# A longer warming, a moved modulation and split products at the opening of a one-core transformer and state-space kernel

## The chip, the core and the metric

The kernel runs on one core of a Trainium2 chip. The metric is the device time of one execution in microseconds. Three runs of the kernel before took 1899.47, 1901.17 and 1896.9 us, with a median of 1899.47. In the text TensorE is PE in the profile (PEld is its loading of weights), VectorE is DVE, ScalarE is ACT, GpSimd is POOL, and the queue that issues the transfers is SP.

## The reference

The reference is a two-layer backbone over 512 latent tokens with a context of 256 tokens, model width 1024. Layer 0 mixes with grouped-query attention, layer 1 with a bidirectional state-space mixer, and a gated feed-forward layer with a short convolution follows each. Every sub-layer starts with a root-mean-square norm and a modulation (a shift and a scale that depend on a condition vector):

```python
silu_c = jax.nn.silu(c)
silu_cc = jax.nn.silu(c_ctx)
...
    mod_l = jnp.split((silu_c @ ada_w[i] + ada_b[i])[:, None, :], 6, axis=-1)
    mod_c = jnp.split(silu_cc @ ada_w[i] + ada_b[i], 6, axis=-1)
    h_l = modulate(rms_norm(x, norm_mix_w[i]), mod_l[0], mod_l[1])
    h_c = modulate(rms_norm(ctx, norm_mix_w[i]), mod_c[0], mod_c[1])
...
q_l, k_l, v_l = jnp.split(h_lat @ w_qkv, [Q_DIM, Q_DIM + KV_DIM], axis=-1)
```

The change touches only the first of these: the norm and modulation of the latent tokens and of the context in layer 0, and the products `h_lat @ w_qkv` for the first six blocks of 128 columns of queries and keys.

## The kernel before

Activations lie transposed: 1024 features are eight tiles of 128 partitions, and a tile has a column for each token, 512 of latents and 256 of context. Precision comes from splitting every operand into a high part of reduced precision (type fp32r) and a low part that is the rest. A product of two such operands is three matmuls, high by high, weight high by activation low and weight low by activation high (`mm3`, lines 105, 106 and 108). ScalarE makes a high part by a copy, and VectorE or GpSimd the low part by a subtraction (`split`, lines 85 and 87).

The function `attention` writes the order of TensorE, ScalarE and VectorE by hand for the opening; the engines run their instructions in the order of the code. The opening goes like this:

- Transfers are queued on SP: the latents X, the parameters, then for each of eight feature tiles a block of modulation weights (`wada`, 1 MB in three pieces) and a slab of projection weights (`wst`, 128 x 768), with a table of constants (`cst`, which holds the identity) and the context in between. SP's order follows the program and isn't changed by the diff.
- TensorE runs 24 products of a tile of ones (line 541, `warm`), whose result nobody reads. In the profile each 128 x 128 product of plain fp32 is two records.
- ScalarE squares the eight latent tiles, VectorE adds them to `acc`, and TensorE sums that over partitions (line 274, `ss`). `rstd_rows` then makes the reciprocal root by a logarithm and an exponential on ScalarE and small VectorE steps, spreads it to `rba` (line 285) and turns it by four transposes (line 291, `rsT`).
- `ada` makes the shift and scale of one feature tile in stages, at each `next`: eight products of 32 columns (line 128, `ps_ada`) and a copy of their result by VectorE (line 130, `ada_sb`); then two products that turn it (line 134, `ps_adt`), and in `modulation` two additions of 128 x 2 (line 145, `mod`) and the gain (line 148, `moda`). The bodies of `ada` and `modulation` aren't changed.
- `modulated` applies them: VectorE makes `ht` (line 319), ScalarE the high part `hha` (line 328), VectorE the low part `hla` (line 329).
- The main loop runs over eight k-steps m, one for each feature tile. A k-step is six products of 128 x 512 outputs in three parts each (`k_step`, 18 matmuls into six accumulators `ps_l`). In front of its first product stands ps_ada of tile m + 1; behind its second stand ps_adt, the modulation and `modulated` of tile m + 1. The slab of tile m + 1 is split in the k-step m, by ScalarE and, for the first seven, by GpSimd.
- The context's norm is woven in: in the k-steps 1 and 2 four squares each on ScalarE (line 584) with their adds on VectorE (line 586), ahead of the k-step's products; in k-step 3 the sum over partitions, in k-step 4 its transposes, ahead of the products; from k-step 4 on, two context tiles are modulated in each step behind its second product.

k-step 0 differs in one thing: its own modulation is made ahead of the loop, so TensorE waits there for hha. ps_ada of tile 1 stands in that wait.

Of the kernel before, what the change touches and what calls it, by code (L numbers as in the profile page):

```python
# [7 lines left out]
P = 128  # L8
F32 = mybir.dt.float32
F32R = mybir.dt.float32r  # L10
AF = mybir.ActivationFunctionType
ALU = mybir.AluOpType
# [3 lines left out]
D = 1024  # L16
KT = D // P
L = 512
C = 256
# [48 lines left out]
def t3(g, name, dt=F32, n=T):  # L68
    return g.t3p.tile([P, n], dt, tag="t3", bufs=g.n3, name=name)
# [195 lines left out]
def rstd_rows(g, sq, n, cols, width, name, bank):  # L265

    nc = g.nc
    c = cols.shape[-1]  # L270
    nt = n // P
    ps = bank(f"ss{name}")
    for t in range(nt):
        nc.tensor.matmul(ps[:, t * c : (t + 1) * c], sq[:, t * P : (t + 1) * P], cols, start=True, stop=True)
    small = lambda nm: g.p.tile([P, nt * c], F32, tag="rst", bufs=8, name=nm)
    a, y, u = small("rsa"), small("rsy"), small("rsu")
    nc.vector.tensor_scalar(a, ps[:, : nt * c], 1.0 / width, EPS, ALU.mult, ALU.add)

    for f in ((lambda: nc.scalar.activation(y, a, AF.Ln)), (lambda: nc.scalar.activation(y, y, AF.Exp, scale=-0.5))):
        follow(g, f()) if g.tables else f()  # L280
    nc.vector.tensor_tensor(u, y, a, ALU.mult)
    nc.vector.scalar_tensor_tensor(u, y, -0.5, u, ALU.mult, ALU.mult)
    rb = t3(g, f"rb{name}", n=n)
    wide = lambda v: v.unsqueeze(2).broadcast_to([P, nt * c, P // c])
    nc.vector.scalar_tensor_tensor(rb.rearrange("p (a b) -> p a b", b=P // c), wide(u), 1.5, wide(y), ALU.add, ALU.mult)
    yield BREAK
    out = []
    for t0 in range(0, nt, 4):
        pt = bank(f"rsT{name}")
        for t in range(t0, min(nt, t0 + 4)):  # L290
            nc.tensor.transpose(pt[:, (t - t0) * P : (t - t0 + 1) * P], rb[:, t * P : (t + 1) * P], g.ident)
        yield (pt, t0 * P, min(n, (t0 + 4) * P))
# [20 lines left out]
def modulated(g, hl, x, rs, a, b, layer, ca, cb, v, m, pool=False):  # L313

    nc = g.nc
    n = b - a
    t = t3(g, "ht", n=n)
    for ap, c0, c1 in parts(x[m], a, b):
        nc.vector.scalar_tensor_tensor(t[:, c0:c1], ap, g.moda[layer][ca][:, m, v : v + 1], rs[:, c0:c1],  # L319
                                       ALU.mult, ALU.mult)  # L320
    bias = g.mod[layer][cb][:, m, v : v + 1]
    hi, lo = (h[:, a:b] for h in hl)
    if pool:
        nc.scalar.activation(t, t, AF.Identity, bias=bias)
        nc.scalar.copy(hi, t)
        nc.gpsimd.tensor_tensor(lo, t, _r(hi), ALU.subtract)
        return
    nc.scalar.activation(hi, t, AF.Identity, bias=bias)
    nc.vector.scalar_tensor_tensor(lo, t, bias, _r(hi), ALU.add, ALU.subtract)
# [160 lines left out]
def attention(g, adas, project, X):  # L490


    nc, I = g.nc, g.I
    S64 = slice(0, 64), slice(64, 128)
    Bk, Sb = (lambda name: Bank(g, name)), (lambda name: S(g, name))
    t2 = lambda name, dt=F32: g.t3p.tile([P, 512], dt, tag="t2", bufs=6, name=name)
    g.h = [[htiles(g, n, f"a{i}_{m}") for m in range(KT)] for i, n in enumerate((L, C))]
    hl, hc = g.h
# [8 lines left out]
    slabs = []  # L507
# [29 lines left out]
                nc.sync.dma_start(X[:, a : a + 4, L:], I["ctxT"][a * P : (a + 4) * P].rearrange("(k p) t -> p k t", p=P))  # L537

    warm = Bk("warm")
    for _ in range(24):  # L540
        nc.tensor.matmul(warm[:, :P], g.ones, g.ones, start=True, stop=True)
    acc = t3(g, "acc", n=L)
    for m in range(KT):
        sq = t2("sql") if m else acc
# [14 lines left out]
                            e.rearrange("p (k v) -> p k v", v=2), ALU.mult)  # L559
    next(norm)  # L560
    next(mods[0])
    rsl, _, _ = next(norm)
    next(mods[0])
    next(loads[0], None)
# [6 lines left out]
    def k_step(m, j, out, h):  # L571
        ks = slice(j * P, (j + 1) * P)
        mm3(g, tuple(w[:, ks] for w in slabs[m]), [(out, h[m])], m == 0, m == KT - 1)

    for m in range(KT):
        if 1 <= m < KT - 5 + 1:
            next(mods[m + 5 - 1])
            next(loads[m + 5 - 1])
        if m == 1:
            sqc = t3(g, "sqc", n=C)  # L580
        if m in (1, 2):
            for a in range(4 * m - 4, 4 * m):
                sq = t2("sqc")[:, :C] if a else sqc
                nc.scalar.activation(sq, xs[1][a], AF.Square)
                if a:
                    nc.vector.tensor_tensor(sqc, sqc, sq, ALU.add)
        if m == 3:
            norm = rstd_rows(g, sqc, C, g.ones[:, :1], D, "a", Bk)
            next(norm)
        if m == 4:  # L590
            rsc = t3(g, "rsc", n=C)
            pt, _, _ = next(norm)
            nc.scalar.copy(rsc, pt[:, :C])
        for j in range(6):
            if m + 1 < KT and j == 0:
                next(mods[m + 1])
            k_step(m, j, pl[j], hl)
            if m + 1 < KT:
                if j == 0:
                    next(loads[m + 1], None)  # L600
                if j == 0 + 1:
                    next(mods[m + 1])
                    modulated(g, hl[m + 1], xs[0], rsl, 0, L, 0, 1, 0, 0, m + 1)
            if m >= 4 and j == 1:
                for a in (2 * m - 8, 2 * m - 7):
                    modulated(g, hc[a], xs[1], rsc, 0, C, 0, 1, 0, 1, a, pool=True)
    for _ in mods:
        next(_, None)
    man.__exit__(None, None, None)
# [1036 lines left out]
```

## Time and profile before

| what | value |
|---|---|
| runs, median of three | 1899.47 us (1896.9 to 1901.17) |
| the profiled execution | 1901.27 us |
| its span from first to last instruction | 1899.3 us |
| mean granted TensorE clock | 0.995 |
| TensorE busy, 0 to 10 us and 10 to 15 us | 7.40 and 3.13 us |
| first product of the k-steps 0, 1, 2 and 3 | 19.45, 28.15, 33.98, 41.50 us |

Everything in the prediction is read from one profiled execution. A row of the order in time gives the start, how long it took from the first to the last of a group, the engine, the line, the operation, the tile written and those read, and how often; in brackets stands the idle time ahead of it and what ended it. A row of a stretch gives its bounds and length and then, for each engine, its busy time and the number of instructions, at last the granted TensorE clock as a share of full speed, the share of the transfer engines and GB/s. Records of consecutive matmuls overlap: their distance from start to start is what one costs in a stream.

### The profile page before, as it was taken

What the parts mean: (1) busy time and instruction counts of PE and PEld (TensorE: products, weight loads), DVE (VectorE), ACT (ScalarE), POOL (GpSimd) and SP (SyncE); (2) the same over time, 40 slices, a digit from 0 to 9 for tenths busy, and PEclk for the clock granted to TensorE, in tenths of its full rate; (3) what the DMA queues carried; (4) which work ended last, traced back from release to release, by engine and by line L of the source; (5) the groups of instructions that cost most, each with busy time, mean ns of one, the idle gap of its engine ahead of it and who ended that gap; (6) DMA issues with size and microseconds to landing.
All of it is one profiled execution on the core that took longest, in us unless ns stands there. A gap on an engine that the chain in (4) does not pass through costs nothing.

```text
span 1899.3 us, 27264 instructions
## 1 busy us (share of the span) xinstructions
PE 1863.7 (98%) x10696; PEld 1526.5 (80%) x10696; DVE 1335.2 (70%) x1989; ACT 841.9 (44%) x1450; POOL 251.3 (13%) x236
## 2 busy tenths in 40 slices
PE   8999999989999999999989999999999999999999
PEld 6864545588888888888888888888888888888887
DVE  4588989678777777544488777777878576565655
ACT  3654544354122222222266777766667353323331
POOL 2200000031000000000040344443335200000000
PEclk8999999999999999999999999999999999999999
DMA  9223341014433555222123444444344323323232
GB/s 340 67 70 108 102 149 61 2 56 169 140 123 117 175 188 178 67 67 67 56 90 89 119 118 115 124 121 132 113 131 118 98 77 104 102 85 111 89 100 89
DMA packets 73424, 210.00 MB, mean 111 GB/s; under 512 B 8912, under 2 KB 14416, under 8 KB 73168
## 3 DMA queue, kind: packets, MB, share of 16 engines
q1 hardware_dynamic: 73296, 208.26, 35.7%
q8 instruction: 84, 1.38, 0.3%
q14 instruction: 44, 0.36, 0.1%
HBM read 198.79 MB, written 6.82 MB: 108 GB/s over the span
## 4 chain that ended last, share of the span: by engine, by line
PE 80%; DVE 11%; issue 4%; ACT 3%; DMA 1%; POOL 1%; SPq 0%; DVEq 0%; POOLq 0%; ACTq 0%
PE ps_up L105 10%; PE ps_up L106 10%; PE ps_up L108 10%; PE ps_d L105 6%; PE ps_d L108 6%; PE ps_d L106 6%; PE ps_in L108 4%; PE ps_in L106 4%; PE ps_in L105 4%; PE ps_o L771 2%; PE ps_s L807 2%; PE ps_st L1233 2%; DVE ht L319 1%; PE ps_wo L108 1%; PE ps_wo L105 1%
## 5 line engine op out<-in xcount | busy, mean ns | idle before, releaser
L87 DVE TENSOR_TENSOR wl<-wst,wh 128x1024 fp32r<-128x1024 f32 x211 | 263.5, 1249 | 233.0 <-PE ps_up L106 117.2
L85 ACT CAST wh<-wst 128x1024 fp32r<-128x1024 f32 x211 | 221.2, 1049 | 413.0 <-DMA wst<-in_wup 319.2
L106 PE MATMUL ps_up<-hlf,wh 128*128 128x512 f32 x1008 | 357.0, 354 | 0.0
L108 PE MATMUL ps_up<-hhf,wl 128*128 128x512 f32 x1008 | 356.8, 354 | 0.0
L105 PE MATMUL ps_up<-hhf,wh 128*128 128x512 f32 x1008 | 356.6, 354 | 0.0
L105 PEld LDWEIGHTS ps_up<-hhf,wh 128*128 128x128 f32 x1008 | 190.6, 189 | 26.5
L106 PEld LDWEIGHTS ps_up<-hlf,wh 128*128 128x128 f32 x1008 | 190.7, 189 | 26.3
L108 PEld LDWEIGHTS ps_up<-hhf,wl 128*128 128x128 f32 x1008 | 190.5, 189 | 26.4
L105 PE MATMUL ps_in<-hhs,wh 128*128 128x512 f32 (+1 forms) x560 | 204.4, 365 | 0.0
L106 PE MATMUL ps_in<-hls,wh 128*128 128x512 f32 (+1 forms) x560 | 199.4, 356 | 0.0
L108 PE MATMUL ps_in<-hhs,wl 128*128 128x512 f32 (+1 forms) x560 | 198.7, 355 | 0.0
L105 PE MATMUL ps_d<-hdh,wh 128*128 128x512 f32 (+1 forms) x568 | 193.5, 342 | 1.4 <-DVE X L981 1.2
L108 PE MATMUL ps_d<-hdh,wl 128*128 128x512 f32 (+1 forms) x568 | 193.3, 341 | 0.0
L106 PE MATMUL ps_d<-hdl,wh 128*128 128x512 f32 (+1 forms) x568 | 193.0, 340 | 0.3 <-DVE hdl L87 0.3
L981 DVE SCALAR_TENSOR_TENSOR X<-ps_d,mod,X 128x512 f32<-128x512 f32 (+1 forms) x224 | 125.1, 585 | 33.9 <-PE ps_d L108 33.3
L106 PEld LDWEIGHTS ps_d<-hdl,wh 128*128 128x128 f32 x568 | 106.7, 188 | 14.9 <-DVE hdl L87 0.7
L105 PEld LDWEIGHTS ps_d<-hdh,wh 128*128 128x128 f32 x568 | 106.3, 188 | 14.8 <-DVE X L981 1.4
L105 PEld LDWEIGHTS ps_in<-hhs,wh 128*128 128x128 f32 x560 | 105.9, 189 | 15.1 <-issue 1.0
L108 PEld LDWEIGHTS ps_in<-hhs,wl 128*128 128x128 f32 x560 | 105.8, 189 | 14.8
L108 PEld LDWEIGHTS ps_d<-hdh,wl 128*128 128x128 f32 x568 | 106.7, 188 | 13.1
L106 PEld LDWEIGHTS ps_in<-hls,wh 128*128 128x128 f32 x560 | 106.0, 189 | 13.2
L810 ACT ACTIVATE pr<-ps_s 128x1024 f32<-128x1024 f32 x56 | 57.2, 1021 | 99.0 <-PE ps_s L809 91.0
(353 smaller groups left out, 3496.0 us busy)
## 6 DMA issues: line engine op xcount, KB each, us to landing
wst<-in_wup SPq DMA_DIRECT2D x88, 512.0 KB, 3.6
wada<-in_adaT SPq DMA_DIRECT2D x56, 512.0 KB, 3.7
wst<-in_win SPq DMA_DIRECT2D x48, 512.0 KB, 3.7
wst<-in_wdown SPq DMA_DIRECT2D x44, 512.0 KB, 3.7
E<-ad SPq DMA_DIRECT2D x64, 256.0 KB, 6.7
wada<-in_adaB SPq DMA_DIRECT2D x24, 512.0 KB, 5.0
ec<-ead SPq DMA_DIRECT2D x64, 128.0 KB, 5.4
wst<-in_wout SPq DMA_DIRECT2D x16, 512.0 KB, 3.7
```

The costliest lines, as they stand in the source:

```text
L85: keep(nc.scalar.copy(hi, src))
L87: keep(eng.tensor_tensor(lo, src, _r(hi), ALU.subtract))
L105: mm(out, wh, ah, start=first, stop=False)
L106: mm(out, wh, al, start=False, stop=False)
L108: mm(out, wl, ah, start=False, stop=last)
L319: nc.vector.scalar_tensor_tensor(t[:, c0:c1], ap, g.moda[layer][ca][:, m, v : v + 1], rs[:, c0:c1], ALU.mult, ALU.mult)
L771: nc.tensor.matmul(po[S64[e], :n], v, pr[:, 512 * e + off : 512 * e + off + n], start=first, stop=last)
L807: nc.tensor.matmul(outs[e], a[S64[e], k], b[S64[e], q], start=i == 0, stop=False)
L810: nc.scalar.activation(pr, ps, AF.Exp)
L981: nc.vector.scalar_tensor_tensor(ap, o[:, c0:c1], gate[:, m, v : v + 1], ap, ALU.mult, ALU.add)
L1233: nc.tensor.matmul(ps[:, d * 256 : (d + 1) * 256], Bt[:, t * P : (t + 1) * P], xw[d][t], start=t == ts[0], stop=t == ts[-1])
```

## The change

Four edits, all in the opening:

1. 38 warming products instead of 24, and four more between ps_ada of tile 0 and the four transposes.
2. In k-step 0 ps_ada of tile 1, which stood ahead of the first product, stands ahead of the third column block, and ps_adt with what follows it behind the fourth block.
3. In k-step 0 the two products with the high part of the activations (hha) run for all six column blocks first, then the six with its low part (hla). The accumulators get the same 18 terms.
4. The context's squares come two blocks later, behind ps_adt and the modulation of the next tile, and the sum over partitions, its transposes and the modulation of context tiles move by one to three blocks inside their k-steps.

```diff
                 nc.sync.dma_start(X[:, a : a + 4, L:], I["ctxT"][a * P : (a + 4) * P].rearrange("(k p) t -> p k t", p=P))

     warm = Bk("warm")
-    for _ in range(24):
-        nc.tensor.matmul(warm[:, :P], g.ones, g.ones, start=True, stop=True)
+
+    def busy(n):
+        for _ in range(n):
+            nc.tensor.matmul(warm[:, :P], g.ones, g.ones, start=True, stop=True)
+
+    busy(38)
     acc = t3(g, "acc", n=L)
     for m in range(KT):
         sq = t2("sql") if m else acc
@@ -559,6 +563,7 @@
                             e.rearrange("p (k v) -> p k v", v=2), ALU.mult)
     next(norm)
     next(mods[0])
+    busy(4)
     rsl, _, _ = next(norm)
     next(mods[0])
     next(loads[0], None)
@@ -572,38 +577,49 @@
         ks = slice(j * P, (j + 1) * P)
         mm3(g, tuple(w[:, ks] for w in slabs[m]), [(out, h[m])], m == 0, m == KT - 1)

+    def squares(a0):
+        for a in range(a0, a0 + 4):
+            sq = t2("sqc")[:, :C] if a else sqc
+            nc.scalar.activation(sq, xs[1][a], AF.Square)
+            if a:
+                nc.vector.tensor_tensor(sqc, sqc, sq, ALU.add)
+
+    sqc = t3(g, "sqc", n=C)
     for m in range(KT):
         if 1 <= m < KT - 5 + 1:
             next(mods[m + 5 - 1])
             next(loads[m + 5 - 1])
-        if m == 1:
-            sqc = t3(g, "sqc", n=C)
-        if m in (1, 2):
-            for a in range(4 * m - 4, 4 * m):
-                sq = t2("sqc")[:, :C] if a else sqc
-                nc.scalar.activation(sq, xs[1][a], AF.Square)
-                if a:
-                    nc.vector.tensor_tensor(sqc, sqc, sq, ALU.add)
-        if m == 3:
-            norm = rstd_rows(g, sqc, C, g.ones[:, :1], D, "a", Bk)
-            next(norm)
-        if m == 4:
-            rsc = t3(g, "rsc", n=C)
-            pt, _, _ = next(norm)
-            nc.scalar.copy(rsc, pt[:, :C])
+        first = 2 if m == 0 else 0
         for j in range(6):
-            if m + 1 < KT and j == 0:
+            if m + 1 < KT and j == first:
                 next(mods[m + 1])
-            k_step(m, j, pl[j], hl)
+            if m:
+                k_step(m, j, pl[j], hl)
+            else:
+                ks = slice(j * P, (j + 1) * P)
+                for w in slabs[0]:
+                    nc.tensor.matmul(pl[j], w[:, ks], hl[0][0], start=w is slabs[0][0], stop=False)
             if m + 1 < KT:
-                if j == 0:
+                if j == first:
                     next(loads[m + 1], None)
-                if j == 0 + 1:
+                if j == first + 1:
                     next(mods[m + 1])
                     modulated(g, hl[m + 1], xs[0], rsl, 0, L, 0, 1, 0, 0, m + 1)
-            if m >= 4 and j == 1:
+            if m in (1, 2) and j == 2:
+                squares(4 * m - 4)
+            if m == 3 and j == 2:
+                norm = rstd_rows(g, sqc, C, g.ones[:, :1], D, "a", Bk)
+                next(norm)
+            if m == 4 and j == 0:
+                rsc = t3(g, "rsc", n=C)
+                pt, _, _ = next(norm)
+                nc.scalar.copy(rsc, pt[:, :C])
+            if m >= 4 and j == 2:
                 for a in (2 * m - 8, 2 * m - 7):
                     modulated(g, hc[a], xs[1], rsc, 0, C, 0, 1, 0, 1, a, pool=True)
+        if m == 0:
+            for j in range(6):
+                nc.tensor.matmul(pl[j], slabs[0][0][:, j * P : (j + 1) * P], hl[0][1], start=False, stop=False)
     for _ in mods:
         next(_, None)
     man.__exit__(None, None, None)
```

On TensorE's queue the opening stood before like this, from the warming to the first three products (ssa is the sum over partitions, rsTa the transposes, hha_0_102 and hla_0_103 the two parts of tile 0, wsh and wsl those of the slab; the product of the plain type counts once here):

```order
L541 MATMUL warm<-ones 128x128 x24
L274 MATMUL ssa<-ones,acc 128x1 x4
L128 MATMUL ps_ada<-wada,sc_83 32x256 x8
L291 MATMUL rsTa<-cst,rba 128x128 x4
L134 MATMUL ps_adt<-cst,ada_sb 128x2 x2
L128 MATMUL ps_ada<-wada,sc_83 32x256 x8
L105 MATMUL ps_l<-hha_0_102,wsh 128x512
L106 MATMUL ps_l<-hla_0_103,wsh 128x512
L108 MATMUL ps_l<-hha_0_102,wsl 128x512
```

With the change the same place reads:

```order
L543 MATMUL warm<-ones 128x128 x38
L274 MATMUL ssa<-ones,acc 128x1 x4
L128 MATMUL ps_ada<-wada,sc_83 32x256 x8
L543 MATMUL warm<-ones 128x128 x4
L291 MATMUL rsTa<-cst,rba 128x128 x4
L134 MATMUL ps_adt<-cst,ada_sb 128x2 x2
L601 MATMUL ps_l<-hha_0_102,wsh 128x512
L601 MATMUL ps_l<-hha_0_102,wsl 128x512
L601 MATMUL ps_l<-hha_0_102,wsh 128x512
L601 MATMUL ps_l<-hha_0_102,wsl 128x512
L128 MATMUL ps_ada<-wada,sc_83 32x256 x8
```

The second ps_ada moved from ahead of the first product to behind the fourth, and no product near the front reads hla.

On ScalarE's queue, from the split of the slab of tile 1 to the high part of tile 4, the difference is (sqc are the context's squares, wsh the high part of a slab; - is before, + with the change):

```order
 L85 CAST wsh<-wst 128x768
 L328 ACTIVATE hha_1_104<-ht,mod_86 128x512
-L584 ACTIVATE sqc<-X 128x256 x4
 L85 CAST wsh<-wst 128x768
 L328 ACTIVATE hha_2_106<-ht,mod_86 128x512
-L584 ACTIVATE sqc<-X 128x256 x4
+L583 ACTIVATE sqc<-X 128x256 x4
 L85 CAST wsh<-wst 128x768
 L328 ACTIVATE hha_3_108<-ht,mod_86 128x512
+L583 ACTIVATE sqc<-X 128x256 x4
+L85 CAST wsh<-wst 128x768
+L328 ACTIVATE hha_4_110<-ht,mod_86 128x512
```

Each group of four squares moved from behind one tile's high part to behind the next one's, and it still stands between a high part and the cast of a slab.

On VectorE's queue, at the modulation of tile 2, the difference is:

```order
 L319 SCALAR_TENSOR_TENSOR ht<-X,moda_98,rsl 128x512
 L329 SCALAR_TENSOR_TENSOR hla_2_107<-ht,mod_86,hha_2_106 128x512
-L586 TENSOR_TENSOR sqc<-sqc 128x256 x4
+L585 TENSOR_TENSOR sqc<-sqc 128x256 x3
 L130 COPY ada_sb<-ps_ada 128x256
 L145 TENSOR_TENSOR mod_86<-ps_adt,par 128x2
```

The second group of adds, four of them, left this place, and the first group, three adds, took it; both stand ahead of a copy of ada_sb, as before.

## The prediction, made blind

> **What bounds the kernel now.** I read the page first, then the granted clock by stretches, then the order of time on each engine up to 64 us, the only part where the change moves anything.
>
> ```profile
> span 1899.3 us, 27264 instructions
> PE 1863.7 (98%) x10696; PEld 1526.5 (80%) x10696; DVE 1335.2 (70%) x1989; ACT 841.9 (44%) x1450; POOL 251.3 (13%) x236
> PE 80%; DVE 11%; issue 4%; ACT 3%; DMA 1%; POOL 1%; SPq 0%; DVEq 0%; POOLq 0%; ACTq 0%
> ```
>
> TensorE bounds the whole run, so a microsecond by which its stream starts earlier should reach the end. I therefore price one number: when the first product of the second k-step starts (28.15 us now). From there on both kernels have the same products.
>
> The stretches below are cut where the granted clock (PEclk) changes, which is only at multiples of 3.41 us from each other.
>
> ```profile
> core 0: us, PE busy (x) PEld busy (x) DVE busy (x) ACT busy (x) POOL busy (x), PEclk, DMA share, GB/s
> 1.39:4.81 3.42, 3.42 (x17) 3.42 (x17) 0.00 (x0) 1.16 (x3) 0.00 (x0) 1.00 0.87 266
> 4.81:8.22 3.41, 3.41 (x33) 3.41 (x31) 2.08 (x3) 2.21 (x5) 0.00 (x0) 1.00 1.03 372
> 8.22:11.63 3.41, 0.23 (x3) 0.04 (x1) 2.58 (x4) 2.26 (x5) 0.00 (x0) 1.00 0.96 298
> 11.63:15.05 3.42, 3.18 (x24) 2.38 (x24) 1.52 (x10) 1.05 (x3) 0.47 (x2) 0.50 1.05 409
> 18.46:21.87 3.41, 3.22 (x13) 1.65 (x6) 1.27 (x3) 1.93 (x3) 1.19 (x1) 0.50 1.04 377
> 21.87:25.29 3.42, 3.42 (x12) 2.85 (x11) 1.14 (x4) 0.57 (x1) 0.63 (x1) 0.50 1.08 375
> 25.29:28.70 3.41, 3.41 (x27) 2.13 (x26) 2.33 (x5) 2.10 (x6) 1.23 (x1) 1.00 1.03 397
> 434.89:438.30 3.41, 2.22 (x16) 1.81 (x15) 3.00 (x5) 1.62 (x4) 2.28 (x2) 1.00 0.00 0
> 165.23:168.65 3.42, 2.58 (x14) 1.65 (x14) 3.30 (x6) 1.00 (x2) 0.00 (x0) 1.00 0.00 0
> 168.65:172.06 3.41, 3.41 (x13) 2.12 (x11) 1.92 (x3) 0.00 (x0) 0.00 (x0) 0.50 0.00 0
> ```
>
> Seventeen warming records fill the first stretch and 33 the next, so the first ran at half clock too (the column starts with its first record, at 4.81). The stretch 8.22 to 11.63 held 0.23 us of products, and from 11.63 to 25.29 the clock is 0.50. It returns after a stretch that was full (3.42), not after one with 3.22. The work of the opening pays for that:
>
> ```profile
> 1.05 7.40 PE L541 MATMUL warm<-ones 128*128 128x128 f32 x48 [1.05 <-DVE ones L1488]
> 11.87 1.87 PE L274 MATMUL ssa<-ones,acc 128*128 128x1 f32 x8 [3.42 <-DVE acc L547]
> 13.67 1.93 PE L128 MATMUL ps_ada<-wada,sc 128*32 128x256 f32 x16
> 15.64 1.12 PE L291 MATMUL rsTa<-cst,rba 128*128 128x128 f32 x4
> 16.55 0.85 PE L134 MATMUL ps_adt<-cst,ada_sb 128*128 128x2 f32 x4
> 17.33 1.93 PE L128 MATMUL ps_ada<-wada,sc 128*32 128x256 f32 x16
> 19.45 0.79 PE L105 MATMUL ps_l<-hha,wsh 128*128 128x512 f32 x1 [0.19 <-ACT hha L328]
> 25.66 0.39 PE L105 MATMUL ps_l<-hha,wsh 128*128 128x512 f32 x1
> 26.82 0.40 PE L108 MATMUL ps_l<-hha,wsl 128*128 128x512 f32 x1
> 27.15 1.07 PE L128 MATMUL ps_ada<-wada,sc 128*32 128x256 f32 x16
> 28.15 0.50 PE L105 MATMUL ps_l<-hha,wsh 128*128 128x512 f32 x1
> 29.65 0.50 PE L134 MATMUL ps_adt<-cst,ada_sb 128*128 128x2 f32 x4
> 40.07 0.50 PE L274 MATMUL ssa<-ones,sqc 128*128 128x1 f32 x4
> 166.09 1.05 PE L134 MATMUL ps_adt<-cst,ada_sb 128*128 128x2 f32 x8 [0.84 <-DVE qsq L662]
> ```
>
> At full clock a product follows the last by (26.82 - 25.66)/5 = 0.23 us; ps_ada takes 1.07 instead of 1.93.
>
> **The change, part by part.**
>
> *38 warming products for 24.* Fourteen more are 28 records at 3.41/31 = 0.11 us: the warming ends at 8.45 + 3.1 = 11.55 instead of 8.45. The sum waits for acc until 11.87, so nothing is late, the hole shrinks from 3.4 to 0.3 us, and the clock should stay full at 11.63. Then ssa takes about 0.95 (twice the 0.50 of the row with x4) instead of 1.87, and everything behind it comes 0.9 earlier: the transposes, which wait for rba, can start at 14.7 instead of 15.64. If the clock comes up later than at 4.81 (the stretches need not lie the same in every execution), up to 1.0 us of warming runs into ssa; the next part says why this too costs little.
>
> *Four more between ps_ada and the transposes.* 8 x 0.11 = 0.9 us, from about 13.85 (ps_ada starts at 12.8 and takes 1.07) to 14.75, while VectorE makes rba: 0.1 at most. Transposes and ps_adt then take about 0.45 and 0.35, the modulation (L145) can start at 15.65, its scale moda (L148) is due at 15.95 instead of 17.70: 1.75 us won, on paper.
>
> *What is late next.* POOL's split of the first slab stands there:
>
> ```profile
> 14.33 0.51 POOL L713 COPY id<-cst 64x64 f32<-64x64 f32 x2 [13.89 <-DMA cst<-in_cst]
> 15.27 1.98 POOL L87 TENSOR_TENSOR wsl<-wst,wsh 128x768 fp32r<-128x768 f32 x1 [0.43 <-POOL id L713]
> 17.43 0.23 DVE L145 TENSOR_TENSOR mod<-ps_adt,par 128x2 f32<-128x2 f32 x2 [1.32 <-PE ps_adt L134]
> 17.70 0.16 DVE L148 SCALAR_TENSOR_TENSOR moda<-mod,par 128x2 f32<-128x2 f32 x1
> 19.43 0.75 DVE L329 SCALAR_TENSOR_TENSOR hla<-ht,mod,hha 128x512 fp32r<-128x512 f32 x1 [0.79 <-ACT hha L328]
> 55.46 1.84 POOL L87 TENSOR_TENSOR wsl<-wst,wsh 128x768 fp32r<-128x768 f32 x1
> 55.70 1.62 DVE L148 SCALAR_TENSOR_TENSOR moda<-mod,par 128x2 f32<-128x2 f32 x1
> 34.19 1.85 POOL L87 TENSOR_TENSOR wsl<-wst,wsh 128x768 fp32r<-128x768 f32 x1 [4.88 <-ACT wsh L85]
> 32.87 3.45 DVE L586 TENSOR_TENSOR sqc<-sqc 128x256 f32<-128x256 f32 x4
> 36.24 0.41 DVE L130 COPY ada_sb<-ps_ada 128x256 f32<-128x256 f32 x1
> ```
>
> At 55.70 the same moda took 1.62 us instead of 0.16: it ends at 57.32, when POOL's split that began at 55.46 ends (57.30). So does the last of four adds at 34.45. Both read two SBUF tiles. POOL's first split hangs on transfers (cst lands at 14.33), not on the clock: it stays at 14.9 to 15.3 and ends between 16.7 and 17.25. Moda is held until then, 17.05 as my value, and the first product follows as now (19.45 - 17.86 = 1.59): at 18.65, only **0.8 us earlier**. A delay of ssa by up to 1.0 disappears in the same hold.
>
> The Trainium skill, "SBUF — State Buffer", section "Who interferes with whom", has a rule that speaks against this part: a VectorE instruction with two SBUF inputs contends with a GpSimd instruction that reads SBUF, and the later one blocks fully. The two rows at 55 us agree; by the rule 0.8 us is won here, without it 1.75.
>
> *The second modulation inside the first k-step.* Its ps_ada (17.33) now runs in a hole and costs nothing; inside the step it costs 1.1 us of product time at full clock, and the hole, from the end of ps_adt (15.8) to 18.65, is empty. What the wait for hla costs now (second product 0.78 instead of 0.43 behind the first) goes with the low parts last: 0.35 won. The first step at full clock is then 18 x 0.233 + 1.1 + 0.37 (ps_adt) + 1.1 (next ps_ada) = 6.77 us, and the second modulation is in time: its ps_adt ends 3.4 us after the start, and from there hha took 2.0 and hla 2.75 us (17.43 to 19.43 and 20.18), so they are ready at 5.4 and 6.2. Together: 18.65 + 6.77 = **25.4**, if the clock holds.
>
> *Does it hold?* By the transposes' end TensorE has no product for 3.3 us. The stretch 165.23 to 168.65 was busy for 2.58 us, 1.05 of these with ps_adt, which moves two columns, and the clock fell behind it; one with 2.22 us of wide products (434.89) kept it. In the profiled position the stretch 15.05 to 18.46 would hold some 0.3 us of products; wherever the grid lies, some stretch takes in 1.8 us or more of such a hole. I take a fall at 17 to 20.3 and one stretch at half clock. With the fall at 18.46 and a full stretch after it, 3.2 us of the step run at half speed: 1.6 lost, 27.0. Over the grid's positions the loss runs from 1.5 to 2.8 (a second stretch, where the first isn't full); I take 1.7: **27.1 against 28.15, 1.05 us won**. Ends: 0 and 3.3 (half clock to the end of the step).
>
> The Trainium skill, "TensorE: Matmul & The Clock Gate", Part 1, has the clock fall after a whole idle window of about 3.4 us, which this hole doesn't contain. The row at 165.23, with under 1 us idle at a time, speaks against it; by that rule nothing would be lost.
>
> *The squares behind the turnings.* On ScalarE and VectorE the two groups only move one step later; what follows each is the same: squares, the cast of a slab, POOL's split; adds, the copy of ada_sb. The stall
>
> ```profile
> 36.71 0.61 PE L134 MATMUL ps_adt<-cst,ada_sb 128*128 128x2 f32 x4 [1.06 <-DVE ada_sb L130]
> 33.30 0.82 ACT L85 CAST wsh<-wst 128x768 fp32r<-128x768 f32 x1
> ```
>
> came from ada_sb (36.24 to 36.65), which stands behind the fourth add, and that was held by the split that started 0.26 us before it, right behind the cast. The same four stand ahead of the same kind of cast one step later, so the 1.06 us moves from the third to the fourth k-step: zero. If the add slips ahead of POOL: 1.06 won. ssa and the transposes of the context move inside steps at their old cost; the context's rows come before the fifth step's modulations in both orders. DMAs are issued in the same order, and from 45 us on none is open.
>
> **Sum.** 0.8 (first product) + 0.35 (hla) - 1.1 (ps_ada moved in) + 1.2 (half clock: 5.8 us from 19.45 to 25.29 cost 2.9 now, 1.7 then) gives 1.25; by the two starts it is 1.05, and I keep that. The profiled execution took 1901.27 us (span 1899.3 and 2.0 around it); it would take 1900.2. It lies 1.8 above the median of the runs, 1899.47; against that: **1898.4**.
>
> **Rivals.**
> - *The clock stays full.* For it: no stretch would be as empty as 8.22 to 11.63 was, with its 0.23 us. Against: 165.23. Second step at 25.4: 2.75 won, 1896.7.
> - *Moda isn't held* (POOL later or quicker than I think). First product at 17.7, a hole of 2.0 us in which the clock falls in fewer positions: second step at 24.5 to 25.5, 2.7 to 3.7 won; with the squares' stall gone as well 4.7: 1896.8 to 1894.8. Against: two rows at 55 us.
> - *Slower: the moved ps_ada is paid at half clock.* If the fall comes 0.4 us or more before the first product, the next stretch isn't full (the 3.22 of now wasn't enough) and the whole step runs at half: 18.65 + 6.77 + 3.3 = 28.7, 0.55 lost: 1900.0. It decides where a stretch ends between 17.0 and 18.2.
> - *The warming doesn't do what it says*: the clock falls at 11.63 all the same. The first product is at 19.45 and the step as in the last rival: 1900.7. Little speaks for it, since the stretch would be full to 11.55.
>
> **How the numbers follow.** Forecast 0.48, full clock 0.19, no hold 0.14, slower 0.16, warming without effect 0.03. Within 0.2% means 3.8 us, about what a measurement of this kernel can tell from no change. Only the third, and not all of it, passes that on the fast side; half a microsecond of the fourth doesn't on the slow one. With the runs of before spread over 4.3 us (1896.9 to 1901.17) I give faster 0.15, same 0.82, slower 0.03. The range takes the no-hold end and the slower rivals with that spread: 1895.3 to 1900.8.
>
> **What would show it.** Right: warming to about 11.5, clock 1.00 from 4.8 to past 17; moda at L148 taking about 1 us; first product near 18.6; one half-clock stretch around it; second step near 27; the idle before ps_adt of 1 us in the fourth step. Wrong: moda at 0.16 with a first product under 18, no 0.50 behind 5 us, or no such stall.

## The result and the profile after

The changed kernel takes 1901.78 us (median of 22 runs, 1898.53 to 1908.05), the kernel before 1899.38 in the same comparison (22 runs, 1896.47 to 1902.4). The ratio is **1.0014, 95% interval 1.0008 to 1.0020**: 2.7 us slower, between 1.5 and 3.8. The forecast was 1898.4 with a range up to 1900.8, so it was wrong in the sign and beyond its range, though the change is still within the 0.2% that the prediction called the same. Yet the execution that was profiled took 1900.13 us, and the forecast for it, before the step to the median, was 1900.2. Why both are true at once is what the rest is about.

First the opening of the changed kernel on TensorE, from the order of time on that engine (start, length, line, operation, then in brackets the idle time ahead and who ended it):

```profile
1.05 10.36 PE L543 MATMUL warm<-ones 128*128 128x128 f32 x76 [1.05 <-DVE ones L1504]
11.51 1.05 PE L274 MATMUL ssa<-ones,acc 128*128 128x1 f32 x8
14.93 0.51 PE L134 MATMUL ps_adt<-cst,ada_sb 128*128 128x2 f32 x4
18.28 0.80 PE L601 MATMUL ps_l<-hha,wsh 128*128 128x512 f32 x1 [2.85 <-ACT hha L328]
20.29 1.65 PE L128 MATMUL ps_ada<-wada,sc 128*32 128x256 f32 x16
26.77 0.50 PE L105 MATMUL ps_l<-hha,wsh 128*128 128x512 f32 x1
41.68 0.61 PE L134 MATMUL ps_adt<-cst,ada_sb 128*128 128x2 f32 x4 [1.57 <-DVE ada_sb L130]
```

The warming reaches to 11.41, ssa takes 1.05 instead of 1.87, and the first product starts at 18.28 (19.45 before). In front of it TensorE is idle for 2.85 us. The second k-step starts at 26.77; 27.1 was forecast. The last row is the one to remember: the idle ahead of ps_adt in the fourth k-step is 1.57 us, where 1.06 was forecast.

VectorE, POOL and ScalarE at the two places, from the order of time on each:

```profile
14.88 1.80 POOL L87 TENSOR_TENSOR wsl<-wst,wsh 128x768 fp32r<-128x768 f32 x1
15.73 0.96 DVE L148 SCALAR_TENSOR_TENSOR moda<-mod,par 128x2 f32<-128x2 f32 x1
36.52 1.32 ACT L583 ACTIVATE sqc<-X 128x256 f32<-128x256 f32 x4
37.32 0.42 DVE L585 TENSOR_TENSOR sqc<-sqc 128x256 f32<-128x256 f32 x1
38.25 3.04 DVE L585 TENSOR_TENSOR sqc<-sqc 128x256 f32<-128x256 f32 x3 [0.51 <-ACT sqc L583]
38.65 1.83 POOL L87 TENSOR_TENSOR wsl<-wst,wsh 128x768 fp32r<-128x768 f32 x1 [3.98 <-PE ps_ada L128]
```

Moda takes 0.96 us and ends with POOL's split (16.68), as forecast (17.05 was put for that end). Of the four adds, the second starts 0.51 us behind the end of the first. The row names ScalarE's squares, but these were done at 37.84 (36.52 + 1.32), and the add starts at 38.25, so most of this wait, 0.41 us, isn't ScalarE's. The third add is then held by POOL's split, and the fourth and the copy of ada_sb stand behind it. Before, three adds got in ahead of the split.

And the clock, from the stretches between which it changes (length, busy time of PE, PEld, DVE, ACT and POOL with counts, granted clock, share of the DMA engines, GB/s):

```profile
11.25:14.67 3.42, 3.32 (x36) 2.60 (x35) 2.33 (x11) 1.18 (x3) 0.51 (x2) 1.00 1.05 408
14.67:18.08 3.41, 0.76 (x8) 0.68 (x6) 1.96 (x5) 0.64 (x2) 1.87 (x2) 1.00 1.04 393
18.08:21.49 3.41, 3.21 (x16) 1.76 (x20) 0.75 (x1) 1.46 (x3) 1.66 (x1) 0.50 1.04 381
21.49:24.91 3.42, 3.42 (x23) 2.60 (x16) 1.57 (x5) 0.17 (x1) 0.17 (x1) 1.00 1.08 373
38.56:41.97 3.41, 1.84 (x9) 1.22 (x9) 2.85 (x4) 0.01 (x1) 1.83 (x1) 1.00 1.04 399
41.97:45.39 3.42, 3.42 (x19) 2.78 (x19) 1.96 (x6) 0.93 (x2) 0.00 (x0) 1.00 0.64 241
```

One stretch at half clock behind the empty one, as forecast; the stretch with the idle of 1.57 us passed without a fall. This profile, in short, shows most of the forecast's steps. It turned out to be the one profile of six in which the clock does not fall behind the idle of 1.57 us.

That it also met the forecast time is luck. The forecast had 1.05 us won at the second k-step and kept to the end. In this profile 1.38 us are won there (26.77 against 28.15), and at the seventh k-step 0.77 are left (58.46 against 59.23). From there on it goes by what no step of the forecast had: falls of the clock (at 148 and 169 us in before, at 165 in after) and later waits. The same product comes 2.33 us before its like at 252.44 us (254.77 in before) and 1.19 at 333.66 (334.85), and the span at the end is 1.14 us shorter (1898.17 against 1899.31).

### The profile page after: what moved, and what is told of

The parts are those of the page before. It is cut to its first block, busy times and chain, and to the rows that moved or that the text cites. A ratio compares the mean times of both kernels' runs of the same rounds, so it can differ in the third digit from the quotient of the medians.

```text
span 1898.2 us, 27334 instructions
## 1 busy us (share of the span) xinstructions
PE 1861.0 (98%) x10732; PEld 1526.3 (80%) x10732; DVE 1335.6 (70%) x1989; ACT 841.9 (44%) x1450; POOL 254.1 (13%) x236
## 3 DMA queue, kind: packets, MB, share of 16 engines
q8 instruction: 84, 1.38, 0.3%
## 4 chain that ended last, share of the span: by engine, by line
PE 80%; DVE 10%; issue 3%; ACT 3%; DMA 2%; POOL 1%; SPq 0%; DVEq 0%; POOLq 0%; ACTq 0%
PE ps_up L105 10%; PE ps_up L106 10%; PE ps_up L108 10%; PE ps_d L105 6%; PE ps_d L108 6%; PE ps_d L106 6%; PE ps_in L108 4%; PE ps_in L106 4%; PE ps_in L105 4%; PE ps_o L787 2%; PE ps_s L823 2%; PE ps_st L1249 2%; DVE ht L319 1%; PE ps_wo L108 1%; PE ps_wo L105 1%
## 5 line engine op out<-in xcount | busy, mean ns | idle before, releaser
L105 PEld LDWEIGHTS ps_up<-hhf,wh 128*128 128x128 f32 x1008 | 190.5, 189 | 26.5
```

The lines of the kernel that those rows point to most:

```text
L105: mm(out, wh, ah, start=first, stop=False)
```

## The experiments

All ratios are against the kernel before, with 95% intervals.

**Both kernels once more.** No edit.

> The kernel before, timed once more as a measure of the spread. Both theories: ratio 1.000 to its own earlier runs within 0.001. The question it answers is how much half clock its executions hold: the profiled one held 20.5 us (mean clock 0.995). If the other executions show 0.995 to 0.996 as well, the half clock is usual in it; if they show 0.997 or 0.998, that profile was an unusual one and the forecast of 28.15 as the start of the second k-step was too late for most executions.

> The changed kernel once more, beside the next three on the same chip, for a second profile of it. Clock theory: 2 to 3 us slower than before, mean clock 0.996 to 0.998 in its executions; in the profile a fall of the clock between 17 and 20 us, with one stretch of half clock where it comes after 18.3 and two where it comes sooner (second k-step at 26.8 and 28.5 us).

Before: 1898.8 us, ratio 1.0001 (0.9991 to 1.0012). After: 1900.02 us, ratio 1.0009 (1.0000 to 1.0018). The loss is there again, on the edge of its interval. The second profile of the changed kernel showed a second stretch at half clock, from 43.3 us.

**One part alone, on the kernel before.** The warming (38 and 4), the squares' new place, and the moved modulation:

```diff
# e3 (the lines that make the helper busy are left out)
-for _ in range(24):
-    nc.tensor.matmul(warm[:, :P], g.ones, g.ones, start=True, stop=True)
+busy(38)
...
+busy(4)
# e4 (the steps of the context's norm move with it, as in the change)
-if m in (1, 2):        # ahead of the products
+if m in (1, 2) and j == 2:
+    squares(4 * m - 4)
# e9
+first = 2 if m == 0 else 0
-if m + 1 < KT and j == 0:
+if m + 1 < KT and j == first:
... (in the same way at the slab's split and at ps_adt)
```

> The kernel before with 38 warming products and the four more, nothing else of the change: ps_ada of the second tile stays in the hole ahead of the first product. Clock theory: ps_ada fills that hole, the clock stays full in most executions, the first product is near 18.3 and the second k-step at 24.5 to 25: 2 to 3.5 us faster than before. If the warming itself is what costs (it runs past the point where acc is ready in executions whose clock comes up late): 0.5 to 1 us slower than before.

> The kernel before with the fourth edit alone (the context's squares, their sum, transposes and the context's modulation behind the turnings). Clock theory: no difference from before beyond the stall of ps_adt, which moves from the third to the fourth k-step and grows from 1.06 to 1.57 us: 0 to 0.5 us slower. Order theory: this part carries the loss, 2 to 3 us slower than before.

> The kernel before with nothing changed but the place of the second modulation (moved from ahead of the first product to behind the third). Theory now (the emptied place and the step that takes the product's time are the loss): the first k-step takes the 16 ps_ada products into its stream and is 1.0 to 1.9 us longer, the place ahead of the first product is empty for 2.2 to 3.5 us and the clock falls or stays down there; slower than before by 1 to 3 us, ratio 1.0005 to 1.0016. Rival (the loss needs the longer warming, because only then is there a full clock to lose): the clock is at half through the opening as in the kernel before, only the ps_ada itself is added, ratio 1.000 to 1.0004.

Warming alone: 1898.05 us, 0.9999 (0.9991 to 1.0008). Squares alone: 1898.45, 1.0001 (0.9990 to 1.0011). Modulation alone: 1898.89, 1.0002 (0.9993 to 1.0011). None of them can be told from no change, and none is the loss by itself. For the warming 2 to 3.5 us of gain were expected: a miss. The squares' idle was to grow to 1.57 us and stayed at 1.06, in the fourth k-step: a miss too. In e9 the ratio is that of its rival, though its interval takes in part of the theory's as well, and the clock is at half from 12.7 to 22.9 us, as the rival says. The profile of the warming alone started its second k-step at 24.53 (28.15 before) and lost part of it at the next wait: its idle ahead of ps_adt was 1.31 us, and the clock fell behind it (35.7 to 39.2). More of it was lost at 333 us; the end of the next part comes to that.

**One part taken out of the changed kernel.** The moved modulation put back (e6), the warming (e7), the squares (e8); and the empty place filled with 12 warming products (e2):

```diff
# e6
-first = 2 if m == 0 else 0
+first = 0
# e7
-busy(38)
+busy(24)
...
-busy(4)
# e8
-if m in (1, 2) and j == 2:
+if m in (1, 2):        # ahead of the products, as before
     squares(4 * m - 4)
# e2
 next(mods[0])
+pl = [Sb("ps_l") for _ in range(2)]        # moved up from below
+for _ in range(12):
+    nc.tensor.matmul(pl[0][:, :P], g.ones, g.ones, start=True, stop=True)
 next(loads[0], None)
```

> The changed kernel with the second ps_ada back ahead of the first product (second edit undone, the other three kept). Clock theory: ps_ada fills 15.4 to 17.2 of the hole, the clock stays full through the first k-step in most executions, mean clock 0.998 to 0.999, 2.5 to 4 us faster than the changed kernel, so 0 to 1 us faster than before. Order theory (high parts first, late squares): no gain over the changed kernel.

> The changed kernel with the 24 warming products of before and without the four (first edit undone, the other three kept). Clock theory: half clock from about 11.6 to 25 as before, but with ps_ada inside the half-clock step: the second k-step at 28.5 to 29.5, 0.5 to 2 us slower than before, so no worse than the changed kernel. If the warming is what costs in the changed kernel: as fast as before.

> The changed kernel with the context's squares and what hangs on them in their old places (fourth edit undone, the other three kept). Clock theory: 0 to 0.5 us faster than the changed kernel, so still 1.5 to 3 us slower than before. Order theory: as fast as before.

> The changed kernel with twelve more warming products behind ps_adt, in the 2.85 us in which TensorE waits for the first hha; nothing else differs. Clock theory (the changed kernel is slow because the clock falls in this hole and stays low for one or two stretches of 3.41 us of products): the clock stays full through the first k-step, the second k-step starts near 25 us, and the kernel is 1.7 to 3.4 us faster than the changed one, so 0 to 1 us faster than before. Order theory (the late squares and the ps_ada inside the step cost): no gain over the changed kernel, still 2 to 3 us slower than before.

Modulation back: 1896.34 us, **0.9987** (0.9978 to 0.9996), faster than either kernel. Warming back: 1901.75, 1.0016 (1.0007 to 1.0025), no better than the changed kernel. Squares back: 1898.58, 1.0000 (0.9991 to 1.0009). Place filled: 1897.8, 0.9994 (0.9986 to 1.0002). With the squares back 1.5 to 3 us of loss were expected to stay; they didn't, which goes against the clock theory, by which the emptied place alone is the loss. So, in these runs, the loss comes with the moved modulation and the moved squares together: without either it is gone. With both kept and the place filled it is gone as well, so it isn't the pair alone either. The rows of e6 on ScalarE, VectorE, POOL and TensorE show what the pair does to the adds:

```profile
34.38 1.32 ACT L583 ACTIVATE sqc<-X 128x256 f32<-128x256 f32 x4
35.18 3.46 DVE L585 TENSOR_TENSOR sqc<-sqc 128x256 f32<-128x256 f32 x4
36.50 1.84 POOL L87 TENSOR_TENSOR wsl<-wst,wsh 128x768 fp32r<-128x768 f32 x1 [3.98 <-PE ps_ada L128]
39.02 0.61 PE L134 MATMUL ps_adt<-cst,ada_sb 128*128 128x2 f32 x4 [1.06 <-DVE ada_sb L130]
```

Here the four adds follow each other without the wait, only the last is held, and the idle is 1.06. With the moved modulation in the same kernel (after, e2, e5, e7) it is 1.57 each time.

**Where the half-clock stretches of the changed kernel lie.** The runs list a mean granted clock: 0.99673 over the 22 runs of the changed kernel, 0.99873 over the 11 of e6. A stretch of 3.41 us at half clock is 0.0009 of such a mean, so the changed kernel has about two more of them than e6, and its profile on record showed one in the opening. No edit; four more profiles (e13 to e16), with one expectation:

> The changed kernel, profiled again. Theory A (a second fall behind the idle of 1.57 us in the fourth k-step): half clock once between 17 and 24, and in about half of such profiles once more between 42 and 48; the start of the values at 89 or, with the second, 91. Theory B (a longer stay at the first product): two stretches in a row between 16 and 25, the second k-step at 27.5 to 28.7. Theory C (chance falls behind the opening): one stretch at the first product, and two or more between 140 and 400.

> As in the first look: A, half clock once between 17 and 24 and in half of the profiles once between 42 and 48; B, two stretches in a row between 16 and 25; C, one, and two or more between 140 and 400.

> As in the first look: A, half clock once between 17 and 24 and in half of the profiles once between 42 and 48; B, two stretches in a row between 16 and 25; C, one, and two or more between 140 and 400.

> As in the first look: A, half clock once between 17 and 24 and in half of the profiles once between 42 and 48; B, two stretches in a row between 16 and 25; C, one, and two or more between 140 and 400.

All four have a fall behind the idle in the fourth k-step, at 41.4 to 42.5 us, where theory A had it in about half. The one at the first product, which A had in all, is missing in two (e14, e15). What C says is seen too: falls between 140 and 340 us, two each in e14 and e16, one in e13, none in e15. From e14, the orders of time on VectorE and TensorE, and the stretches:

```profile
37.14 3.03 DVE L585 TENSOR_TENSOR sqc<-sqc 128x256 f32<-128x256 f32 x3 [0.51 <-ACT sqc L583]
40.56 0.61 PE L134 MATMUL ps_adt<-cst,ada_sb 128*128 128x2 f32 x4 [1.57 <-DVE ada_sb L130]
```

```profile
14.11:17.52 3.41, 2.30 (x25) 1.85 (x16) 2.35 (x8) 0.83 (x2) 2.30 (x3) 1.00 1.03 393
37.94:41.35 3.41, 1.84 (x11) 1.27 (x10) 2.61 (x5) 0.00 (x0) 1.42 (x1) 1.00 1.04 393
41.35:44.77 3.42, 3.42 (x12) 2.84 (x11) 2.02 (x8) 1.41 (x4) 0.00 (x0) 0.51 0.84 320
```

The same program, and the stretches lie elsewhere: here the empty place (2.21 us) is split over two of them and costs nothing, while the idle of 1.57 us and the 0.61 of ps_adt lie in one, and the clock falls. In the profile on record that ps_adt starts at 41.68, so half of it falls into the next stretch (from 41.97), and nothing happened.

All profiles of the opening together, by the idle ahead of ps_adt (or of its like one step earlier):

| idle | profiles | a fall right behind it |
|---|---|---|
| 1.57 us | after, e2, e5, e7, e13 to e16 | 6 of 8 (not: after, e2; e13 two stretches) |
| 1.28 to 1.31 us | e3, e8, e9 | 1 of 3 (e3) |
| 1.06 us | before, e1, e4, e6, e11 | 0 of 5 |
| 0.43 us or none | e10, e12, e17, e18 | 0 of 4 |

The price can be read between the starts of the fourth and the sixth k-step: 14.19 us without the fall (after), 15.75 to 15.76 with one stretch (e5, e14, e15, e16), 17.28 with two (e13), and 13.68 in e6. At the first product, from the first to the second k-step, it is 7.02 to 7.03 us without a fall (e14, e15) and 8.49 to 8.56 with one (after, e5, e13, e16).

**The squares' idle taken away.** Two squares to a k-step over four k-steps, with the steps of the context's norm one to four column blocks later; in e10 on e6's kernel, in e17 on the changed kernel, where the empty place stays:

```diff
-    for a in range(a0, a0 + 4):
+    for a in range(a0, a0 + 2):
...
-if m in (1, 2) and j == 2:
-    squares(4 * m - 4)
+if m < 4 and j == 2:
+    squares(2 * m)
```

> The changed kernel with its second modulation left inside the first k-step and the context's squares two to a k-step. Theory (behind the idle of 1.57 us the clock falls in most executions): the idle and the fall behind it go, the emptied place at the first product stays; 2 to 3 us faster than the changed kernel, 1898 to 1899.3, ratio 0.9995 to 1.0002, half clock at the first product in about two of three executions and nowhere between 25 and 60. Rival (the emptied place alone is the loss): the ratio stays above 1.0008.

> The changed kernel with the second modulation put back, and the context's squares two to a k-step over four k-steps instead of four over two. Theory (the idle before ps_adt comes from a fourth add that is still held by POOL's split when ada_sb should be copied): with one or two adds to a step the copy of ada_sb is not late, the idle of 1.06 us ahead of ps_adt in the fourth k-step is gone, and no clock fall lies behind it in any execution; 1 to 1.5 us faster than the kernel with the second modulation put back (1896.3), so 1894.8 to 1895.4, ratio 0.9979 to 0.9982. Rival (something else than the adds holds that step, or the adds of the other steps are now held): no gain, 1896.3, ratio 0.9987, with an idle of about 1 us ahead of a ps_adt or of a first product in another step.

e17: 1897.5 us, **0.9994** (0.9986 to 1.0003). Its stretches at the first product and in the fourth k-step:

```profile
14.78:18.20 3.42, 0.62 (x8) 0.54 (x5) 1.96 (x5) 0.83 (x2) 1.76 (x1) 1.00 1.03 393
18.20:21.61 3.41, 3.41 (x20) 1.68 (x20) 0.68 (x1) 1.20 (x2) 1.81 (x1) 0.50 1.05 379
38.68:42.10 3.42, 3.42 (x27) 2.57 (x20) 1.56 (x6) 0.00 (x0) 1.94 (x1) 1.00 1.04 398
```

The empty place and its fall are still there; the idle is gone, and with it the loss: from 1.0014 (1.0009 in the repeat) to 0.9994, 3.8 us (2.9), more than the 2 to 3 expected, or at their upper end. e10: 1896.4, 0.9985 (0.9976 to 0.9993). Its values start 1.28 us earlier than e6's (85.68 against 86.96), but the median is the same as e6's, so the expected 1 to 1.5 us are a miss in the time; it can't be told apart at this spread.

**Is moda held by POOL's split?** A copy of one column of moda on POOL, so that the split has to come behind it; the six products with the slab's low part come behind the six with its high part. In e11 on e6's kernel, in e12 with the squares spread too; in e18 as in e12, with the order on POOL pinned:

```diff
 next(mods[0])
+late = g.const.tile([P, 1], F32, name="late")
+nc.gpsimd.tensor_copy(late, g.moda[0][1][:, 0, 0:1])   # e18: kept in program order
 next(loads[0], None)
```

> The changed kernel with the second modulation put back, and POOL's split of the first slab made to wait for moda (a copy of one column of moda on POOL ahead of it); the products with the low part of the slab come behind the six with the high part, so that none waits for it. Theory (moda is held by that split, 0.92 to 0.96 us instead of 0.16): moda takes 0.16 us, the first product starts 0.7 to 0.8 us after where it would with no hold, at 17.7 to 17.9 instead of 18.6, and the second k-step 0.7 us earlier; 1895.6, ratio 0.998 to 0.9986. Rival (the length of moda in that place is not POOL's doing): moda still takes 0.9 us, the first product stays at 18.4 to 18.6, ratio 0.9987. Second rival (the split only holds the next VectorE instruction with two SBUF tiles instead, hla): hla ends 0.8 to 1 us late, but its products come last and nothing waits; the gain is the same.

> The squares spread over four k-steps and the late split together, on the changed kernel with the second modulation put back. Both theories: the gains add, as they lie in different places on TensorE's stream: 1.7 to 2.2 us faster than that kernel, 1894.1 to 1894.6, ratio 0.9975 to 0.9979. Rival (a gain at the opening is given back at the next wait, as with the longer warming alone): no faster than the better of the two alone, ratio 0.998 or above.

> The second modulation put back, the squares spread, and POOL's split of the first slab held behind moda by order (the copy of one column of moda now stands ahead of it). Theory (the split holds moda): moda takes 0.16 us instead of 0.92, the first product comes 0.5 to 0.8 us earlier relative to the end of ps_adt (2.0 to 2.3 us behind it instead of 2.8), and the second k-step with it; 0.9978 to 0.9985, which can't be told from the same kernel without it. Rival: moda still takes 0.7 to 0.9 us.

e11: 1897.3 us, 0.9993 (0.9984 to 1.0002). e12: 1896.21, 0.9986 (0.9977 to 0.9994). Neither tests the hold: the copy was placed behind the split (17.06 and 15.16 in e11), and moda took 0.67 and 0.92 us still. In e12 the two gains were to add up to 1894.1 to 1894.6, a miss as well. In e18 the order is right, on VectorE, POOL and TensorE:

```profile
16.63 0.16 DVE L148 SCALAR_TENSOR_TENSOR moda<-mod,par 128x2 f32<-128x2 f32 x1
17.14 1.82 POOL L87 TENSOR_TENSOR wsl<-wst,wsh 128x768 fp32r<-128x768 f32 x1
18.36 1.15 DVE L329 SCALAR_TENSOR_TENSOR hla<-ht,mod,hha 128x512 fp32r<-128x512 f32 x1 [0.79 <-ACT hha L328]
18.38 0.73 PE L601 MATMUL ps_l<-hha,wsh 128*128 128x512 f32 x2 [1.03 <-ACT hha L328]
```

Moda takes 0.16, and the first product comes 2.04 us behind the end of ps_adt (16.34) instead of 2.80 in e12. The hold is POOL's split. It moved to hla, which took 1.15 instead of 0.75; the copy of ada_sb behind it was late, and in this profile the clock fell there (20.3 to 23.7). 1897.15 us, 0.9989 (0.9980 to 0.9998): nothing won by it.

## Why the prediction was wrong, point by point

- **Warming, ssa, transposes: right.** In the profile on record warming to 11.4, clock 1.00 from 4.45 to 18.1, everything to ps_adt about where it was put.
- **Moda held by the split: right**, 0.96 us, first products at 18.13 to 18.70 in the six profiles (18.65 forecast), and shown by e18. There the rule of the Trainium skill, "SBUF — State Buffer", section "Who interferes with whom", agrees: the two-input instruction that comes second waits, be it moda (0.96 against 0.16) or hla (1.15 against 0.75).
- **The empty place and its fall: right in size on average.** One stretch at half clock in four profiles of six, at 1.5 us each (1.7 was taken). The second k-step started at 26.5 in the mean of the six (27.1 forecast) and at 27.6 in the mean of three profiles of the order before (before, e1, e4): 1.1 us won, against 1.05 forecast. That they agree this well is partly luck: e4 alone starts it at 26.54, before and e1 at 28.15 and 28.22. Nor does some stretch take in 1.8 us of the hole wherever the stretches lie, as the prediction has it. An even split of its 3.3 us leaves 1.65, and in e14, where the clock came up late, the warming ran longer and the hole was 2.21, it left 1.1, and the clock stayed.
- **The squares: this is the step that failed.** The prediction said: "The same four stand ahead of the same kind of cast one step later, so the 1.06 us moves from the third to the fourth k-step: zero." The order on the queues was the same, but with the moved modulation the second add starts 0.51 us behind the first, one add fewer gets in ahead of POOL's split, and the idle is 1.57. With that the clock falls behind it, which it didn't with 1.06. Over the six profiles the term is 0.51 + (4 x 1.57 + 3.09)/6 = **2.1 us lost instead of zero**. With it the opening is 1.0 us slower than before, where it was to be 1.05 faster. Taking the idle away turned 1.0014 (1.0009 in the repeat) into 0.9994 (e17). The row of 165.23 (a wait, a ps_adt, and the clock falls) was used for the place ahead of the first product only; this idle, with a ps_adt right behind it, is the same case and was priced as idle time alone.
- **From one execution to the median.** The forecast took the profiled execution of before as 1.8 us above its median and gave the changed kernel the same offset. The two offsets don't belong together. The profile of before has two falls behind the opening, at 148.2 and 168.7 us; e1, the same kernel with the same opening, has none and lies 1.5 us *below* its median. The profile of after, 1.65 us *below* its median, is the only one of six without a fall behind the idle.
- **The clock's rule.** The Trainium skill, "TensorE: Matmul & The Clock Gate", Part 1, lets the clock fall after a whole idle window. The runs don't agree: stretches that were busy for 1.84 us of 3.41 fell (e14).
- **From the second k-step to the end: a second step that failed.** The prediction let every microsecond of the opening reach the end, with the words "From there on both kernels have the same products." The products are the same, but not their waits. These rows are from before, then from after, on SP and TensorE:

```profile
327.04 0.33 SPq L797 DMA_DIRECT2D odram<-o  x1
327.42 0.43 SPq L95 DMA_DIRECT2D wst<-in_w_o  x1
329.68 0.32 SPq L855 DMA_DIRECT2D od<-odram  x1
334.85 0.50 PE L807 MATMUL ps_s<-qh,kh 64*128 64x512 f32 x2 [0.68 <-ACT pr L810]
324.68 0.33 SPq L813 DMA_DIRECT2D odram<-o  x1
325.06 1.50 SPq L95 DMA_DIRECT2D wst<-in_w_o  x1
327.99 0.32 SPq L871 DMA_DIRECT2D od<-odram  x1
333.66 0.50 PE L823 MATMUL ps_s<-qh,kh 64*128 64x512 f32 x2 [1.89 <-ACT pr L826]
```

SP issues the transfer of od 3.31 us behind that of odram instead of 2.64. ScalarE waits 3.42 us instead of 2.20 for wst and od ahead of pr, and TensorE 1.89 instead of 0.68 for pr. The five kernels without the longer warming (before, e1, e4, e7, e9) have 2.64 to 2.69 us on SP and wait 0.37 to 0.89. Fourteen of the fifteen profiles with it have 3.31 to 3.94 and wait 1.60 to 2.27; e2 is the exception (2.68 and 1.09). At the end of this wait or right behind it the clock fell in five of the fourteen (e3, e5, e10, e13, e16), in none of the six others. So the longer warming, which wins at the opening, goes with a loss of about 1.1 us here, and more where the clock falls. This fits with e3, which gained nothing, and with e7, which lost nothing by leaving it out.

What stays open: the opening explains about 1.0 of the 2.7 us (1.5 to 3.8) of the first comparison and of the 1.7 (0 to 3.4) of the repeat. By the profiles the wait at 333 us adds about 1.0, and the falls behind it, in three of the six, some 0.75 on average. This is an estimate from six profiles of after and two of before, and no run tests it by itself. A wait for wada near 250 us varies as well: 0.5 to 0.6 us in all in before, e1 and e7, 0.9 to 1.8 in the others, so it follows no single edit. Why SP is late with the longer warming isn't shown. Why the second add starts late only when the second modulation was moved isn't settled either: the squares stand at the same distance from the high part in e6 and e14.

## What to carry over

A wait that is moved from one step to the next isn't the same wait: what reaches a queue ahead of a blocking instruction decides it, and half a microsecond more can cost four times as much once the clock falls behind it. So price every idle on TensorE twice, as idle time and as the chance that a stretch around it loses the clock, and remove the longest instead of shifting it. And follow a gain at the start through the later waits: about as much as the warming won was lost again at 333 us. One profile shows one position of the stretches; where a term hangs on them, several profiles of one kernel are worth more than a finer reading of one.

## What the runs showed of the hardware

- **About half a stretch of wide products keeps the clock.** Counted here is the time in which TensorE had a product other than ps_adt and ssa (of one or two columns), in each stretch of 3.41 us at full clock, over all 20 profiles up to some 380 us. The 43 stretches behind which the clock fell hold 0.16 to 1.84 us; of those behind which it stayed, five hold 1.52 to 1.59 and all others 1.71 or more. So below 1.52 it always fell, above 1.84 never, and between these both happened. By that an idle of 1.06 us with its ps_adt (1.88 left in before) stays just above the line, and one of 1.57 (1.37 to 1.46 left where it fell, 1.52 in after) falls in most positions. The profile's busy time alone doesn't tell: 1.84 in both stretches shown above, of after and of e14, without and with a fall.
- **A stretch need not be full for the clock to come back.** It came back behind 3.21 us of work (after, 18.08 to 21.49), and not behind 3.22 (before, 18.46 to 21.87). The prediction's reading, that it takes a full stretch, doesn't hold.
- **The stretches lie differently in each execution.** The first rise of the clock is at 4.45 us in after, 4.85 in e13 and 7.28 in e14 (same program). With 1.5 to 1.6 us for each stretch at half clock on the path, this can make up much of the spread of the runs: 21 of the 22 runs of the changed kernel average 1899.1 us at a mean clock of 0.998, 1901.4 at 0.997 and 1903.0 at 0.996. Near 145 and 165 us the clock fell in some profiles of one kernel and not in others (in before and not in e1, in e14 and not in e15).
